# Moving the stores of two output tensors from SP's queue to ScalarE's, in a hybrid decoder layer

## The chip, the cores and the metric

The kernel runs on one core of one Trainium2 chip. The metric is device time in microseconds of one execution, and lower is better. Engines are named as the profile names them: PE is TensorE (its weight loads are listed apart as PEld), DVE is VectorE, ACT is ScalarE, POOL is GpSimd, and SP is SyncE, which here does nothing but issue DMAs.

## The reference

One decoder layer over 2048 tokens of width 1024, in float32. After a norm, one projection feeds two parallel mixers. The first is a diagonal state-space scan with a gated unit behind it; the second a chunked scan over 16 heads with a gate. Each output is normalised, both go through one output projection with a residual, and a gated feed-forward layer follows. Cut to the two places that the change touches:

```python
def s5_mixer(u, ...):
    ...
    g = jax.nn.gelu(y)
    out = g * jax.nn.sigmoid(g @ w_glu + b_glu)       # gated unit

def ssd_mixer(z, xbc, dt, ...):
    ...
    y = (y_diag + y_off).reshape(bsz, L, SSD_HEADS, SSD_HEAD_DIM) + d_skip[:, None] * xh
    y = y.reshape(bsz, L, SSD_WIDTH) * jax.nn.silu(z)

def reference(...):
    y_a = rmsnorm(s5_mixer(...), s5_norm)
    y_b = rmsnorm(ssd_mixer(...), ssd_norm)
    x = x + jnp.concatenate([y_a, y_b], axis=-1) @ w_out
    h = rmsnorm(x, norm_ffn)
    x = x + (silu(h @ w_gate) * (h @ w_up)) @ w_down
    return rmsnorm(x, norm_final)
```

## The kernel before

Float32 products are made of three fp32r matmuls each (high × high, high × low, low × high), so operands are first split into a high part (a cast on ScalarE) and a low part (a subtraction on VectorE or GpSimd). The stages in order: the input projection of the first half of the tokens; tables for the first mixer; the projection of the second half beside the first mixer's scan; then a long stretch in which the second mixer (`ssd`) runs beside the rest of the projection and then beside the gated unit (`glu`), so that PE always has large matmuls to fill the gaps of the mixer's chain; then the output projection and the feed-forward layer as products by Winograd's scheme (`winograd`, L1141).

The second mixer works through four quarters of 512 tokens. In each there are eight pairs of heads, 32 head pairs in all (`ssd_pair`). One pair loads its gate `sz` (L816) and its input `xs` (L818, three buffers), transposes `xs` on PE (`ps_xt`, L822), makes `xde` and `xdt` on VectorE (L827, L828), state products on PE (`ps_st`, L832) and the running state on VectorE (`PV` and `carry`, L840, after a copy on GpSimd, L835); GpSimd makes decay products (L849) that PE sums (`ps_seg`, L850) and ScalarE turns into `L` (exponential, L852); one more exponential makes `E` (L858). PE then makes `ps_yd` (L863) and `ps_yo` (L867). VectorE puts the output together in the tile `E` (L870 to L873), SP stores it to `ybD` (L874), ScalarE squares it (L878) and GpSimd adds the squares up for the norm (L880). `E` has two buffers.

The gated unit works through two halves of 1024 tokens. At the start of each, sixteen loads bring `gD` into staging tiles (L942, a ring of two buffers, `wst`, which the weights use as well), ScalarE casts (L943) and VectorE subtracts (L944). Then come 16 products per half of 24 matmuls (L81 to L83, `ps_glu`), with the weights split at L64 to L69. For each product SP loads `gs` (L955, four buffers), ScalarE takes a tanh (L961, `sg`, two buffers), VectorE multiplies (L962), SP stores `sg` to `yaD` (L963), ScalarE squares it (L965), and GpSimd or VectorE adds the squares up (L967).

No order is written out by hand for most of this. The program's own scheduler, which plays a timeline of the engines through, places every instruction of an engine in a fixed order; the order is then run in order by each engine, and a DMA that waits holds all that stands behind it in its queue. Two rules tie the stages: the matmuls of the gated unit may not be placed before marks in the head pairs (`issue_after`, `k.marks`), two marks to a pair, and the last four products of the 32 stand behind the last mark. DMAs take eight completion semaphores in turn, over both hardware queues together, and a DMA waits until the last one on its semaphore has landed, where that isn't known from another wait.

The output projection takes its first buffers from the space that the second mixer frees, so its splits (L988 on ScalarE, L993 on VectorE) can't start before the last head pair is done. Its operands: `wA` are pieces of the token tile (L1280) and `wS` sums of them (L1099 to L1105); `s` are pieces of the weights (L1270).

Of the kernel before, what the change touches and what calls it, by code (L numbers as in the profile page):

```python
# [58 lines left out]
def split_w(k, src, n=P, lo_pool=False):  # L59

    nc = k.nc
    kt = src.shape[0] // P
    st = k.wp.tile([P, kt, n], F32, tag="wst", name="wst", bufs=k.wst_bufs)
    nc.sync.dma_start(st, src.rearrange("(k p) n -> p k n", p=P))  # L64
    hi = k.wp.tile([P, kt, n], F32R, tag="whi", name="whi", bufs=2)
    nc.scalar.copy(hi, st)  # L66
    lo = k.wp.tile([P, kt, n], F32R, tag="wlo", name="wlo", bufs=2)
    eng = nc.gpsimd if lo_pool else nc.vector
    eng.tensor_sub(lo, st, hi.bitcast(F32))  # L69
    return hi, lo  # L70


def gemm_cm(k, ps, w, r, behind=None):


    nc = k.nc
    (wh, wl), (rh, rl) = w, r
    n = wh.shape[1]
    for i in range(n):
        with k.tc.issue_after(behind[2 * i // n]) if behind else nullcontext():  # L80
            nc.tensor.matmul(ps, wh[:, i, :], rh[:, i, :], start=(i == 0), stop=False)  # L81
            nc.tensor.matmul(ps, wh[:, i, :], rl[:, i, :], start=False, stop=False)  # L82
            last = nc.tensor.matmul(ps, wl[:, i, :], rh[:, i, :], start=False, stop=(i == n - 1))  # L83
    return last
# [189 lines left out]
def bc(ap, shape):  # L274
    return ap.to_broadcast(shape)
# [532 lines left out]
def ssd_pair(k, q, m, grp, d):  # L808

    nc, sp = k.nc, k.sp  # L810
    V, G = nc.vector, nc.gpsimd
    C, Bt, Gm = grp
    cols = slice(q * 512, q * 512 + 512)
    mp = slice(m * P, m * P + P)
    sz = sp.tile([P, 512], F32, name="sz", bufs=2)
    nc.sync.dma_start(sz, k.zD[mp, cols])  # L816
    xs = sp.tile([P, 512], F32, name="xs", bufs=3)
    nc.sync.dma_start(xs, k.xD[mp, cols])  # L818
    hs = slice(2 * m, 2 * m + 2)
    ps = k.ps_x.tile([P, 4, 2, 64], F32, tag="x", name="ps_xt")  # L820
    for i in range(4):
        t = nc.tensor.transpose(ps[:, i].rearrange("p a b -> p (a b)"), xs[:, i * P : i * P + P], k.ident)  # L822
    k.marks.append(t.ins)
    sh = [P, 4, 2, 64]
    xdt = sp.tile(sh, F32, name="xdt", bufs=2)
    xde = sp.tile(sh, F32, name="xde", bufs=1)
    V.tensor_mul(xde, ps, bc(d.ddt[:, :, hs].unsqueeze(3), sh))  # L827
    V.tensor_mul(xdt, ps, bc(d.dtp[:, :, hs].unsqueeze(3), sh))  # L828

    pst = k.ps_x.tile([P, 4, P], F32, tag="x", name="ps_st")  # L830
    for i in range(4):
        nc.tensor.matmul(pst[:, i, :], Bt[:, i, :], xde[:, i].rearrange("p a b -> p (a b)"), start=True, stop=True)  # L832
    PV = sp.tile([P, 4, P], F32, name="PV", bufs=2)
    st = k.carry[:, m, :]
    G.tensor_copy(PV[:, 0, :], st)  # L835
    for i in range(4):
        for hh in range(2):
            s = slice(hh * 64, hh * 64 + 64)
            et = d.etot[:, i, 2 * m + hh : 2 * m + hh + 1]
            V.scalar_tensor_tensor(PV[:, i + 1, s] if i < 3 else st[:, s], PV[:, i, s], et, pst[:, i, s], op0=MUL, op1=ADD)  # L840

    Ls = []
    for hh in range(2):
        psg = k.ps_x.tile([P, 4, P], F32, tag="x", name="ps_seg")
        for i in range(2):
            r = k.r[:, k.turn % 8]
            k.turn += 1
            part = d.dtas[:, i, :, 2 * m + hh : 2 * m + hh + 1].bitcast(F32)
            G.tensor_mul(r, bc(k.tri.unsqueeze(1), [P, 4, P]), bc(part, [P, 4, P]))  # L849
            nc.tensor.matmul(psg.rearrange("p a b -> p (a b)"), k.strir, r.rearrange("p a b -> p (a b)"), start=(i == 0), stop=(i == 1))  # L850
        L = sp.tile([P, 4, P], F32, name="L", bufs=4)
        nc.scalar.activation(L, psg, AF.Exp)  # L852
        V.tensor_mul(L, L, Gm)
        Ls.append(L)
    pe = k.ps_x.tile([P, 512], F32, tag="x", name="ps_e")
    k.marks.append(nc.tensor.matmul(pe, k.sel[:, m, :], d.ac, start=True, stop=True).ins)
    E = sp.tile([P, 512], F32, name="E", bufs=2)
    nc.scalar.activation(E, pe, AF.Exp)  # L858
    yield
    pyd = k.ps_x.tile([P, 4, P], F32, tag="x", name="ps_yd")  # L860
    for i in range(4):
        for hh, L in enumerate(Ls):
            nc.tensor.matmul(pyd[hh * 64 : hh * 64 + 64, i, :], xdt[:, i, hh, :], L[:, i, :], start=True, stop=True)  # L863

    pyo = k.ps_x.tile([P, 4, P], F32, tag="x", name="ps_yo")
    for i in range(4):
        k.before = nc.tensor.matmul(pyo[:, i, :], PV[:, i, :], C[:, i * P : i * P + P], start=True, stop=True).ins  # L867
    yield
    y = E
    V.tensor_mul(y, E, pyo.rearrange("p a b -> p (a b)"))  # L870
    V.tensor_add(y, y, pyd.rearrange("p a b -> p (a b)"))
    V.scalar_tensor_tensor(y, xs, k.dcol[:, m : m + 1], y, op0=MUL, op1=ADD)
    V.tensor_mul(y, y, sz)  # L873
    nc.sync.dma_start(k.ybD[mp, cols], y)  # L874
    if m == 0:
        k.sums = sp.tile([P, 512], F32, name="sums", bufs=1) if q < 3 else k.mx.tile([P, 512], F32, name="sums", tag="w6", bufs=1)
    sq = PV.rearrange("p a b -> p (a b)") if m else k.sums
    nc.scalar.activation(sq, y, AF.Square)  # L878
    if m:
        G.tensor_add(k.sums, k.sums, sq)  # L880
# [46 lines left out]
def glu(k, ins, half, sp):  # L927

    nc = k.nc
    V = nc.vector  # L930
    w_glu = ins["s5_w_glu"][0]
    g = [[k.slot([P, KD, 512], F32R) for _ in range(2)] for _ in range(2)]

    weights = lambda i: [(m, split_w(k, w_glu[:, m * P : m * P + P], lo_pool=True)) for m in (i, i + 1)]
    pair = weights(0)
    for b in range(2):
        hi, lo = g[b]
        for m in range(0, KD, 2):
            gs = k.wp.tile([P, 2, 512], F32, tag="wst", name="wst", bufs=k.wst_bufs)
            j0 = half * 4 + b * 2  # L940
            for i in range(2):
                nc.sync.dma_start(gs[:, i, :], k.gD[(m + i) * P : (m + i) * P + P, j0 : j0 + 2, :].rearrange("p j c -> p (j c)"))  # L942
            nc.scalar.copy(hi[:, m : m + 2, :], gs)  # L943
            V.tensor_sub(lo[:, m : m + 2, :], gs, hi[:, m : m + 2, :].bitcast(F32))  # L944
    sums = sp.tile([P, 2, 512], F32, name="suma", tag="x1", bufs=2)
    for i in range(0, KD, 2):
        if i:
            pair = weights(i)
        order = [(m, w, b) for m, w in pair for b in range(2)]
        if i == 0 or i == KD - 2:  # L950
            order = [(m, w, b) for b in range(2) for m, w in pair]
        for q, (m, w, b) in enumerate(order):
            gs = sp.tile([P, 512], F32, name="gs", tag="t4", bufs=4)
            part = lambda t: t[m * P : m * P + P, half * 4 + b * 2 : half * 4 + b * 2 + 2, :].rearrange("p j c -> p (j c)")
            nc.sync.dma_start(gs, part(k.gD))  # L955
            ps = k.ps_g.tile([P, 512], F32, tag="g", name="ps_glu")

            n = half * 32 + i * 4 + q * 2
            last = gemm_cm(k, ps, w, g[b], [k.marks[min(63, n + 8 + j)] for j in range(2)])
            sg = sp.tile([P, 512], F32, name="sg", bufs=2)  # L960
            nc.scalar.activation(sg, ps, AF.Tanh, scale=0.5, bias=k.cols[:, C_BGLU + m : C_BGLU + m + 1])  # L961
            V.scalar_tensor_tensor(sg, sg, 1.0, gs, op0=ADD, op1=MUL)  # L962
            nc.sync.dma_start(part(k.yaD), sg)  # L963
            sq = gs if m else sums[:, b]
            nc.scalar.activation(sq, sg, AF.Square)  # L965
            if m:
                (V if half and i == KD - 2 else nc.gpsimd).tensor_add(sums[:, b], sums[:, b], sq)  # L967
            if half and i + q == 1:
                with k.tc.issue_after(last.ins):
                    glu_norm(k, 0, k.suma)  # L970
    k.suma = sums
    if half:
        glu_norm(k, 1, sums)
# [486 lines left out]
def trunk_kernel(ctx, tc, ins, out, dbg=None, upto="all"):  # L1460
# [157 lines left out]
    for half in range(2):  # L1618
        glu(k, ins, half, mx)
# [39 lines left out]
```

## Time and profile before

| | us |
|---|---|
| median of 3 runs | 2890.96 |
| lowest, highest | 2889.64, 2892.86 |
| the profiled execution | 2886.14 |
| its span | 2884.4 |
| PE busy in it | 2767.6 |
| VectorE busy | 1984.5 |
| ScalarE busy | 1127.0 |
| GpSimd busy | 897.8 |
| first and last moved store issued at | 762.3, 1229.5 |

The span runs from the first to the last instruction of the program; the profiled execution's own time is 1.74 us longer. Busy time is what an engine spends in instructions that compute; issuing DMAs is not counted in it. The mean granted clock of PE was 0.985 of full speed. An arrow in a row of waits reads "waited for": the engine, line and tile on the left waited for the one on the right; the numbers are the total in us, how often, and the longest.

### The profile page before, as it was taken

How to read it: one execution, taken by the hardware profiler on the slowest of the kernel's cores; microseconds unless marked ns; L12 is line 12 of the kernel's file. 1: busy time of each engine (PE TensorE's matmuls, PEld its weight loads, DVE VectorE, ACT ScalarE, POOL GpSimd, SP SyncE). 2: the span in 40 equal slices, each digit the busy share in tenths (PEclk: the TensorE clock that was granted, in tenths of full speed). 3: DMA queues.
4: the chain of work that ended last, by engine and by line, in shares of the span. 5: the costliest groups of instructions: out<-in, count | busy, mean ns of one | idle time of the engine just before them, and what ended most of it. 6: DMA issues, size and time to landing. Idle time of an engine off the chain costs nothing. (4 is left out here: it accounts for less than half of the span.)

```text
span 2884.4 us, 36196 instructions
## 1 busy us (share of the span) xinstructions
PE 2767.6 (96%) x13116; PEld 2223.4 (77%) x13116; DVE 1984.5 (69%) x3488; ACT 1127.0 (39%) x1799; POOL 897.8 (31%) x1007
## 2 busy tenths in 40 slices
PE   7999999998999998999998999999999999999998
PEld 6777877676887787888776888887888887878776
DVE  7397319997777888876658655557655556785776
ACT  4234332233555343433435333334333334352443
POOL 2488741212766686300142651021400000000021
PEclk9999999999999999999999999999999999999999
DMA  7378656443445555755664773233532224675653
GB/s 186 94 218 272 227 183 185 147 147 96 127 126 168 172 163 176 252 184 177 192 179 124 238 234 119 81 117 103 197 103 88 75 87 153 238 277 175 219 166 105
DMA packets 337690, 473.39 MB, mean 164 GB/s; under 512 B 34940, under 2 KB 242920, under 8 KB 337512
## 3 DMA queue, kind: packets, MB, share of 16 engines
q1 hardware_dynamic: 303048, 367.00, 40.6%
q0 software_dynamic: 25760, 95.69, 9.9%
q10 hardware_dynamic: 8704, 8.39, 1.0%
q8 instruction: 103, 1.69, 0.2%
q14 instruction: 75, 0.61, 0.1%
HBM read 299.06 MB, written 171.97 MB: 163 GB/s over the span
## 5 line engine op out<-in xcount | busy, mean ns | idle before, releaser
L1141 PE MATMUL ps_w<-s,wS 128*128 128x512 f32 x3936 | 952.8, 396 | 23.7 <-DVE s L993 8.4
L1141 PEld LDWEIGHTS ps_w<-s,wS 128*128 128x128 f32 x3936 | 744.0, 190 | 194.4 <-DVE s L993 10.1
L1141 PE MATMUL ps_w<-s,wA 128*128 128x512 f32 x2952 | 721.2, 394 | 10.0 <-ACT s L988 4.4
L1141 PEld LDWEIGHTS ps_w<-s,wA 128*128 128x128 f32 x2952 | 552.6, 188 | 140.4 <-ACT s L988 7.9
L81 PE MATMUL ps_in<-s,whi 128*128 128x512 f32 x896 | 355.7, 398 | 5.5 <-ACT whi L66 3.0
L83 PE MATMUL ps_in<-s,wlo 128*128 128x512 f32 x896 | 354.1, 397 | 5.3 <-POOL wlo L69 3.7
L82 PE MATMUL ps_in<-s,whi 128*128 128x512 f32 x896 | 355.2, 397 | 0.0
L988 ACT CAST wS<-sum 128x512 fp32r<-128x512 f32 (+1 forms) x336 | 203.9, 611 | 379.6 <-PE ps_w L1141 218.3
L993 DVE TENSOR_TENSOR wS<-sum,wS 128x512 fp32r<-128x512 f32 (+1 forms) x336 | 229.3, 686 | 141.6 <-ACT wS L988 141.0
L988 ACT CAST wA<-s 128x512 fp32r<-128x512 f32 (+1 forms) x252 | 150.1, 610 | 266.6 <-PE ps_w L1141 182.7
L69 POOL TENSOR_TENSOR wlo<-wst,whi 128x1024 fp32r<-128x1024 f32 x52 | 143.9, 2768 | 269.6 <-ACT whi L66 243.0
L1401 POOL DMA_DIRECT2D s<-wdD x21 | 15.7, 751 | 613.3 <-DVE s L993 519.3
L81 PEld LDWEIGHTS ps_in<-s,whi 128*128 128x128 f32 x896 | 169.5, 189 | 47.5 <-issue 5.9
L83 PEld LDWEIGHTS ps_in<-s,wlo 128*128 128x128 f32 x896 | 169.4, 189 | 45.2 <-POOL wlo L69 4.5
L82 PEld LDWEIGHTS ps_in<-s,whi 128*128 128x128 f32 x896 | 169.5, 189 | 39.3 <-issue 5.6
L1150 DVE TENSOR_TENSOR gu<-ps_w,gu 128x512 f32<-128x512 f32 x134 | 92.5, 690 | 139.8 <-PE ps_w L1141 138.2
L993 DVE TENSOR_TENSOR wA<-s,wA 128x512 fp32r<-128x512 f32 (+1 forms) x252 | 167.8, 681 | 10.7 <-ACT wA L988 10.6
L849 POOL TENSOR_TENSOR s<-cm,dtas 128x512 fp32r<-128x512 f32 x128 | 163.1, 1301 | 23.3 <-PE ps_seg L850 23.3
L66 ACT CAST whi<-wst 128x1024 fp32r<-128x1024 f32 x72 | 75.5, 1048 | 177.1 <-PE ps_in L82 121.8
L1158 ACT COPY gu<-ps_w 128x512 f32<-128x512 f32 x134 | 78.4, 585 | 142.8 <-PE ps_w L1141 136.7
L1099 DVE TENSOR_TENSOR sum<-s 128x512 f32<-128x512 f32 (+1 forms) x84 | 57.6, 686 | 101.8 <-DMA s<-ybD 34.4
L1160 DVE TENSOR_TENSOR x<-x,sg 128x512 f32<-128x512 f32 x116 | 80.0, 695 | 63.3 <-ACT sg L1158 36.0
(381 smaller groups left out, 3948.7 us busy)
## 6 DMA issues: line engine op xcount, KB each, us to landing
wst<-in_w_in_dram SPq DMA_DIRECT2D x56, 512.0 KB
s<-in_w_gate_dram SPq DMA_DIRECT2D x22, 1024.0 KB
s<-in_w_up_dram SPq DMA_DIRECT2D x22, 1024.0 KB
wdD<-s POOLq DMA_DIRECT2D x22, 1024.0 KB, 6.2
actD<-gu SPq DMA_DIRECT2D x44, 512.0 KB
woD<-s POOLq DMA_DIRECT2D x16, 1024.0 KB, 7.4
s<-actD SPq DMA_DIRECT2D x16, 1024.0 KB
s<-wdD POOLq DMA_DIRECT2D x14, 1024.0 KB, 9.7
```

What stands on the lines that cost most here:

```text
L66: nc.scalar.copy(hi, st)
L69: eng.tensor_sub(lo, st, hi.bitcast(F32))
L81: nc.tensor.matmul(ps, wh[:, i, :], rh[:, i, :], start=(i == 0), stop=False)
L82: nc.tensor.matmul(ps, wh[:, i, :], rl[:, i, :], start=False, stop=False)
L83: last = nc.tensor.matmul(ps, wl[:, i, :], rh[:, i, :], start=False, stop=(i == n - 1))
L849: G.tensor_mul(r, bc(k.tri.unsqueeze(1), [P, 4, P]), bc(part, [P, 4, P]))
L988: a = k.nc.scalar.copy(op[:, 0], raw)
L993: b = eng.tensor_sub(op[:, 1, part], raw[:, part], op[:, 0, part].bitcast(F32))
L1141: nc.tensor.matmul(ps, a[:, p, i, :], b[:, q, i, :], start=(root == name and i == 0 and p + q == 0), stop=(i == n - 1 and p == 1), skip_gr ...
L1150: V.tensor_add(dst, ps, dst if onto else src)
L1158: nc.scalar.copy(dst, bank[root])
L1160: V.tensor_add(block, block, dst)
```

## The change

Two stores are issued by ScalarE and no longer by SP. Both stand in the program's text right ahead of the square of the same tile. 32 stores of `ybD` and 32 of `yaD`, 256 KB each, are moved.

```diff
@@ ssd_pair
     V.tensor_mul(y, y, sz)
-    nc.sync.dma_start(k.ybD[mp, cols], y)
+    nc.scalar.dma_start(k.ybD[mp, cols], y)
...
     nc.scalar.activation(sq, y, AF.Square)
@@ glu
             V.scalar_tensor_tensor(sg, sg, 1.0, gs, op0=ADD, op1=MUL)
-            nc.sync.dma_start(part(k.yaD), sg)
+            nc.scalar.dma_start(part(k.yaD), sg)
             sq = gs if m else sums[:, b]
             nc.scalar.activation(sq, sg, AF.Square)
```

Since the scheduler places all instructions anew, the order of every engine changes from the first moved store to somewhat behind the last. No instruction of PE, VectorE or GpSimd is added or taken away, and the count of ScalarE's table loads stays at 43.

First ScalarE late in the gated unit, at the last three head pairs. Before, no DMA stands there:

```order
L66 CAST whi<-wst 128x1024
L961 ACTIVATE sg<-ps_glu,cols 128x512
L878 ACTIVATE PV<-E 128x512
L965 ACTIVATE gs<-sg 128x512
L852 ACTIVATE L<-ps_seg 128x512 x2
L858 ACTIVATE E<-ps_e 128x512
L961 ACTIVATE sg<-ps_glu,cols 128x512
L878 ACTIVATE PV<-E 128x512
```

And ScalarE at the same place in the changed program:

```order
L852 ACTIVATE L<-ps_seg 128x512 x2
L858 ACTIVATE E<-ps_e 128x512
L963 DMA yaD<-sg 128x512
L965 ACTIVATE gs<-sg 128x512
L961 ACTIVATE sg<-ps_glu,cols 128x512
L963 DMA yaD<-sg 128x512
L965 ACTIVATE gs<-sg 128x512
L874 DMA ybD<-E 128x512
L878 ACTIVATE PV<-E 128x512
L852 ACTIVATE L<-ps_seg 128x512 x2
L858 ACTIVATE E<-ps_e 128x512
```

Each store stands right in front of the square of its tile here, and the exponentials of the next pair stand behind both; of all 64 stores 57 have their square as the very next instruction.

Then SP at the end of the gated unit and the start of the output projection, as one piece of the difference (`woD` holds the output projection's weights, `yaD` read into `s` is its first token tile):

```order
 L1280 DMA s_10561<-yaD 128x8x256
 L1270 DMA s_10563<-woD 128x4x512 x2
 L1280 DMA s_10561<-yaD 128x8x256
-L963 DMA yaD<-sg 128x512
-L1270 DMA s_10562<-woD 128x4x512
-L955 DMA gs<-gD 128x512
-L1270 DMA s_10562<-woD 128x4x512
-L963 DMA yaD<-sg 128x512
+L1270 DMA s_10562<-woD 128x4x512 x2
 L1328 DMA x_10635<-in_x_dram 128x1024
 L1270 DMA s_10563<-woD 128x4x512
-L963 DMA yaD<-sg 128x512
```

The stores are gone from between the weight loads, and the load of `gs` between them has moved ahead.

Last VectorE in the splits for the first products of the output projection. `wA11` and `wS1` are the token operands of its first two products, `s1`, `s2` and `s3` pieces of the weights. Before:

```order
L993 TENSOR_TENSOR s2_10614<-s6_10563,s2_10614 128x1024
L103 TENSOR_TENSOR nt_9257<-nt_9257,nv_9256 128x4
L993 TENSOR_TENSOR s1_10608<-s6_10563,s1_10608 128x1024
L108 SCALAR_TENSOR_TENSOR yinv_91<-nt_9257,yinv_91 128x4
L993 TENSOR_TENSOR s1_10608<-s6_10563,s1_10608 128x1024
L962 SCALAR_TENSOR_TENSOR sg_10460<-sg_10460,gs_10433 128x512
L102 TENSOR_TENSOR nt_9257<-yinv_91 128x4
L993 TENSOR_TENSOR wA11_10579<-s5_10561,wA11_10579 128x512
L993 TENSOR_TENSOR wS1_10585<-sum_10582,wS1_10585 128x512
```

And VectorE there in the changed program:

```order
L993 TENSOR_TENSOR s1_10608<-s6_10563,s1_10608 128x1024
L967 TENSOR_TENSOR suma_9945<-suma_9945,gs_10433 128x512
L993 TENSOR_TENSOR wA11_10579<-s5_10561,wA11_10579 128x512
L993 TENSOR_TENSOR wS1_10585<-sum_10582,wS1_10585 128x512
L102 TENSOR_TENSOR nt_9257<-ng_9258 128x4
L962 SCALAR_TENSOR_TENSOR sg_10493<-sg_10493,gs_10466 128x512
L993 TENSOR_TENSOR s2_10614<-s6_10563,s2_10614 128x1024 x2
L993 TENSOR_TENSOR wS4_10594<-sum_10591,wS4_10594 128x512
```

`s2` now stands behind `wA11` and `wS1`, where it stood ahead of them. `s3`, the operand of the third product that PE runs there, comes behind all of these in both orders.

On PE the head pairs and the matmuls of the gated unit are interleaved differently. From the last `ps_yo` (L867) to the first `ps_w` (L1141) there were 47 + 76 = 123 matmuls of the gated unit and are now 50 + 46 = 96; ahead of each of the last four head pairs 25 more have been done than before. At the start of the gated unit's second half, the pair that had 33 such matmuls behind its transposes now has 16, and the next one has 47 where it had 32.

## The prediction

> **What bounds the kernel now.** First the head of the page: one engine is nearly always busy.
>
> ```profile
> span 2884.4 us, 36196 instructions
> PE 2767.6 (96%) x13116; PEld 2223.4 (77%) x13116; DVE 1984.5 (69%) x3488; ACT 1127.0 (39%) x1799; POOL 897.8 (31%) x1007
> ```
>
> PE (TensorE) leaves 2884.4 − 2767.6 = 116.8 us idle in all. Then the stretches in which the moved stores run (the first is issued at 762 us, the last at 1229 us). The columns are the stretch, its length, and the busy time of PE, weight loads, DVE, ACT and POOL, with the granted clock and the DMA share at the end.
>
> ```profile
> 740.00:900.00 160.00, 157.56 (x926) 130.38 (x926) 131.48 (x215) 86.42 (x113) 107.33 (x100) 0.99 0.41 122
> 900.00:950.00 50.00, 47.30 (x281) 37.58 (x280) 40.54 (x70) 26.86 (x37) 31.26 (x23) 1.00 0.64 199
> 950.00:1070.00 120.00, 116.23 (x715) 96.60 (x714) 99.87 (x173) 45.03 (x75) 91.45 (x71) 0.99 0.54 161
> 1070.00:1125.00 55.00, 45.91 (x262) 36.49 (x261) 49.56 (x88) 23.20 (x33) 32.70 (x24) 0.97 0.64 191
> 1125.00:1215.00 90.00, 90.00 (x521) 74.72 (x520) 73.08 (x121) 39.36 (x60) 50.84 (x38) 1.00 0.63 207
> 1215.00:1245.00 30.00, 28.51 (x132) 22.98 (x131) 26.33 (x48) 16.72 (x25) 1.58 (x2) 1.00 0.84 295
> ```
>
> PE is idle for 505.00 − 485.51 = 19.5 us here: 2.4 + 2.7 + 3.8 + 9.1 + 0 + 1.5. That is the most that any reordering in this stretch can win, 0.7% of the span, and half of it lies at 1070 to 1125 us, where the second half of the gated unit starts. Last, what PE waits for between 740 and 1240 us (total, times, longest):
>
> ```profile
> PE ps_glu L82 <- DVE s L944: 3.9, 4, 2.2
> PE ps_xt L822 <- DVE carry L840: 3.5, 2, 2.7
> PE ps_yo L867 <- ACT L L852: 3.0, 2, 1.8
> PE ps_xt L822 <- ACT L L852: 2.9, 1, 2.9
> PE ps_glu L81 <- ACT s L943: 2.0, 2, 1.8
> PE ps_w L1141 <- DVE s L993: 1.2, 1, 1.2
> ...
> PE ps_ac L749 <- ACT E L858: 0.5, 1, 0.5
> ```
>
> No DMA is in this list. PE waits for VectorE and ScalarE, so a store that is issued elsewhere can help only through what those two wait for.
>
> **What the move costs on ScalarE.** What one issue takes (shortest/median/longest in ns): the two stores on SP now, then two transfers of one shape, a load on SP and the store that ScalarE already issues.
>
> ```profile
> L874 SPq DMA_DIRECT2D ybD<-E x32: 319/320/1137, 762.3 to 1193.7; - x32
> ...
> L963 SPq DMA_DIRECT2D yaD<-sg x32: 319/320/4651, 938.4 to 1229.5; - x32
> ...
> L534 SPq DMA_DIRECT2D s<-uD x48: 567/572/1456, 418.5 to 584.2; - x48
> ...
> L625 ACTq DMA_DIRECT2D gD<-yg x64: 582/587/1155, 472.3 to 716.2; - x64
> ```
>
> The uD load on SP and the gD store on ScalarE carry 128 KB each in rows of the same cut and take 0.57 and 0.59 us: the issue follows the shape, not the engine. So I take 0.32 us for each moved store, 64 × 0.32 = 20.5 us of ScalarE; the other end, 0.59 each, is 37.8 us. ScalarE is busy for 237.6 of the 505 us, so it has room; what counts is the delay of the work behind each store. The store's main wait is not new on ScalarE: the square right behind it waits for the same VectorE result.
>
> ```profile
> ACT PV L878 <- DVE E L873: 48.3, 15, 4.9
> ACT gs L965 <- DVE sg L962: 36.2, 19, 5.7
> ...
> ACT E L858 <- DMA ybD<-E: 8.8, 7, 2.0
> ...
> POOL sums L880 <- ACT PV L878: 53.5, 18, 8.1
> ```
>
> ScalarE mostly stands ready when E or sg is done (15 and 19 times above), so the store goes out at once and the square starts 0.32 us later. Behind it stand the square, then the two exponentials (L852), E (L858), the tanh (L961) and the weight cast (L66). GpSimd waits for the square (18 times), and its next decay products stand behind that add. PE is held by ScalarE directly in 6 of its waits above (2 + 1 + 2 + 1), and by the state recurrence (L840), which follows GpSimd's copy, in 2. Eight places × 0.32 = 2.6 us if each gets one store in front, 5.1 us with both stores of a pair; nothing if the new order puts them elsewhere. I take +1.5, with 0 and +5.1 as ends. E's buffer is freed by its store (8.8 us of ScalarE waits, 0.5 of them passed on to PE): the store goes out from where ScalarE is instead of where SP is, ±0.5, taken as 0.
>
> There is one new kind of wait. As built, most DMAs also wait for the landing of the one eight places earlier in the program, whichever queue holds it: 33 of the 64 stores on ScalarE now wait for a DMA of SP, and 44 DMAs of SP for a store of ScalarE. In the order the partner stands one to two head pairs earlier, so it should have landed; I take 0 and keep the bad case for the rivals.
>
> **What SP gains.** SP's own waits between 740 and 1240 us, the ones that go (L963, L874) between ones that stay:
>
> ```profile
> SPq L818 <- DVE E L872: 61.3, 20, 7.1
> ...
> SPq L963 <- DVE sg L962: 38.1, 20, 4.4
> ...
> SPq L874 <- DVE E L873: 29.7, 23, 5.2
> SPq L955 <- POOL suma L967: 25.5, 16, 5.2
> ...
> SPq L942 <- DVE s L944: 12.8, 8, 2.6
> ```
>
> SP loses 67.8 us of waits, and the loads behind them (sz L816, gs L955, weights L64, xs L818) may go earlier. But xs still waits for its buffer (61.3 us), gs for its own (25.5), and the loads of gD that feed the gated unit for the two staging buffers that L944 frees (12.8). So freeing SP lets loads run up against their buffers. PE's waits at the two starts of the gated unit (3.9 + 2.0 = 5.9 us) hang on that ring of two; I take −1 of them, with 0 and −5.9 as ends.
>
> [...]
>
> **What the new order costs at the end.** This term weighs most. From the last ps_yo to the first ps_w the order holds 123 matmuls of the gated unit before and 96 now; at each of the last four head pairs 25 more have been done than before. These rows (start, length) show what the old tail covered:
>
> ```profile
> 1186.87 1.16 PE L867 MATMUL ps_yo<-Cc,PV 128*128 128x128 f32 x8
> ...
> 1216.27 0.39 PE L82 MATMUL ps_glu<-s,whi 128*128 128x512 f32 x1
> 1216.50 0.39 PE L83 MATMUL ps_glu<-s,wlo 128*128 128x512 f32 x1
> 1216.72 0.62 PE L1141 MATMUL ps_w<-s,wA 128*128 128x512 f32 x2
> ...
> 1223.63 0.49 PE L1141 MATMUL ps_w<-s,wA 128*128 128x512 f32 x1 [0.26 <-ACT s L988]
> 1225.35 0.98 PE L1141 MATMUL ps_w<-s,wA 128*128 128x512 f32 x3 [1.23 <-DVE s L993]
> ...
> 1191.98 1.67 DVE L873 TENSOR_TENSOR E<-E,sz 128x512 f32<-128x512 f32 x1
> 1195.93 2.79 DVE L962 SCALAR_TENSOR_TENSOR sg<-sg,gs 128x512 f32<-128x512 f32 x1 [2.28 <-ACT sg L961]
> 1198.65 2.35 DVE L993 TENSOR_TENSOR s<-s,s 128x1024 fp32r<-128x1024 f32 x2
> ```
>
> A matmul starts every 0.23 us, so the last pair now ends 25 × 0.23 = 5.75 us later in PE's work, and the tail is as much shorter. The splits for the output projection can't start before that pair ends, and PE already ran into them (0.26 + 1.23 = 1.49 us). Before, the third product found its operand at 1225.35 − 1186.87 = 38.5 us after the last ps_yo began: 11.8 us to the first split, 26.7 of VectorE work. In the new order about 24.5 us of VectorE work stand in front of it (11 half splits, 7 small splits, 5 sums, 5 steps of the gated unit; the estimate uses the old stretch less one L962, two waits and the small steps that moved behind), and the first split should start at 10 to 11.8 us, so it is ready at 34.5 to 36.3. PE arrives at 0.9 + 96 × 0.23 + 0.8 + 24 × 0.23 + 0.8 = 30.1. It waits 4.4 to 6.2 us instead of 1.49: I take +3. The ends are 0 (the splits keep pace) and +5.75 (all of the lost cover).
>
> **The sum.** +1.5 − 1 + 3 = +3.5 us. The profiled execution took 2886.14 us, 2884.4 of them its span, so 2889.6; the three runs had a median of 2890.96, 4.8 above, so the forecast is 2890.96 + 3.5, rounded to 2894. About 0.2%, 5.8 us, is what a measurement can tell from no change: the likeliest is a change too small to see. Its own range goes from 0 − 5.9 + 0 to 5.1 + 0 + 5.75, that is −5.9 to +10.9, or 2885 to 2902.
>
> **Rivals.**
>
> *Slower: the head pairs become ScalarE's chain.* If in the gated stage each pair's two stores (0.64 us) go through to GpSimd, VectorE and PE, because the pair's chain and not PE sets the pace, 16 pairs cost 10.2 us; with the tail +13.2, 2899 against the profiled time and 2904 as a median. A store held by a slow load of SP, with the exponentials behind it, would do the same. For it: 1070 to 1125 us, where PE is busy 45.9 of 55 us and DVE 49.6, and the 18 waits of GpSimd. Against it: 1125 to 1215 us, where PE has no idle time at all. It decides from the point where PE waits at L822 or L867 in most pairs. Chance 0.26.
>
> *Faster: inputs and outputs apart.* If the loads of gD do come sooner, the 5.9 us at the two starts go, and the output projection's loads are no longer held by stores of sg (one held SP for 4651 ns), so the 1.49 us go too: −7.4, 2878.7 and 2884. For it: the 67.8 us of SP's waits. Against it: the buffers above. [...] Chance 0.20.
>
> *Nothing: stores were in nobody's way.* ScalarE's slack hides the issues and the splits keep pace: 2886.1 and 2891. Chance 0.18.
>
> **How the numbers follow.** The forecast has 0.36, of which 0.05 lies beyond +5.8 us. Slower by over 0.2%: 0.25 of the first rival + 0.05 = 0.30. Faster: 0.20. Between: 0.31 + 0.18 + 0.01 = 0.50. The range takes in the faster rival's 2884 with some room for a start that goes wholly, and the slower one's up to just short of its 2904: 2882 to 2903.
>
> **What would show it.** The ScalarE rows of L874 and L963 should read about 320 ns; near 590, the first cost doubles. L878 and L965 should keep their VectorE waits, now in front of the store. PE's wait on L993 at the first ps_w should grow from 1.2 to some 4 or 5 us: if it stays at 1.5, the tail term is wrong. If the waits on L944 and L943 (5.9 us) vanish, the buffers were not what held the loads. If PE's waits at L822 and L867 grow well above their 9.4 us, the slower rival is right.

## The result and the profile after

The changed kernel takes 2904.3 us (median of six runs, 2895.84 to 2913.53), the kernel before 2889.3 on the same chip (six runs, 2887.99 to 2892.86). The ratio is 1.0053, 95% interval 1.0040 to 1.0066: slower by 15 us, where 2894.0 was forecast, within 2882 to 2903.

The profiled execution took 2904.32 us. The head of its page:

```profile
span 2902.4 us, 36173 instructions
...
PE 2778.1 (96%) x13116; PEld 2230.3 (77%) x13116; DVE 1984.6 (68%) x3488; ACT 1127.8 (39%) x1799; POOL 908.5 (31%) x1007
```

The span grew by 18.0 us, in two parts that want different explanations. PE's idle time is 2902.4 − 2778.1 = 124.3 us, 7.5 more than before. PE's busy time grew by 10.5 us for the same 13116 matmuls: they ran slower, though 3.4 of these 10.5 us lie ahead of 740 us, where the two programs are the same. The same stretches as before, with the granted clock third from the end of each row:

```profile
740.00:900.00 160.00, 154.61 (x911) 127.91 (x910) 131.10 (x219) 86.75 (x112) 113.03 (x100) 0.99 0.40 121
900.00:950.00 50.00, 47.62 (x279) 38.61 (x279) 37.38 (x60) 26.13 (x37) 28.98 (x23) 0.97 0.61 189
950.00:1070.00 120.00, 116.29 (x697) 96.02 (x696) 98.30 (x169) 44.07 (x73) 84.45 (x67) 1.00 0.53 155
1070.00:1125.00 55.00, 45.02 (x261) 36.72 (x260) 46.12 (x81) 21.82 (x31) 33.20 (x25) 0.94 0.67 199
1125.00:1215.00 90.00, 89.14 (x532) 73.66 (x531) 70.66 (x117) 35.46 (x56) 55.91 (x42) 1.00 0.54 161
1215.00:1245.00 30.00, 23.51 (x93) 18.01 (x92) 28.12 (x47) 18.95 (x27) 1.58 (x2) 0.89 1.00 352
```

PE is idle for 505.00 − 476.18 = 28.8 us here, 9.3 more. The last row changed most: 6.5 us of idle where 1.5 was, and a clock of 0.89 where 1.00 was. PE's work there, start and length, with the wait ahead of it in brackets (`ps_ss`, L920, is the sum for a norm):

```profile
1223.50 0.73 PE L1141 MATMUL ps_w<-s,wA 128*128 128x512 f32 x2 [0.43 <-ACT wA L988]
...
1225.81 1.05 PE L920 MATMUL ps_ss<-cm,suma 128*128 128x1 f32 x8 [1.06 <-DVE suma L967]
...
1233.39 0.49 PE L1141 MATMUL ps_w<-s,wA 128*128 128x512 f32 x1 [1.76 <-ACT s L988]
1237.12 9.58 PE L1141 MATMUL ps_w<-s,wA 128*128 128x512 f32 x30 [3.24 <-DVE s L993]
```

And the same place in steps of 5 us:

```profile
1230.00:1235.00 5.00, 2.13 (x8) 1.16 (x7) 5.00 (x9) 4.45 (x6) 0.00 (x0) 1.00 1.04 393
1235.00:1240.00 5.00, 2.88 (x7) 2.30 (x8) 5.00 (x9) 1.69 (x2) 0.00 (x0) 0.55 1.07 375
1240.00:1245.00 5.00, 5.00 (x19) 3.98 (x18) 5.00 (x10) 2.54 (x5) 1.58 (x2) 0.77 0.70 217
```

The waits are followed by a clock of 0.55 and 0.77. In the last line PE is busy for all of the 5 us and still slow. The clock record has 0.5 from 1235.5 to 1242.3 us: 1.65 us of that lie inside the last wait, and behind it twelve matmuls start 0.39 to 0.59 us apart, most of them 0.43, where 0.23 is usual, which makes 2.5 us in all. The issues themselves (shortest, median and longest in ns) take nearly what was forecast; the waits on E's store and PE's wait on E are what grew:

```profile
L874 ACTq DMA_DIRECT2D ybD<-E x32: 325/353/357, 763.1 to 1208.1; - x32
L963 ACTq DMA_DIRECT2D yaD<-sg x32: 326/326/353, 944.2 to 1238.9; - x32
```

```profile
POOL sums L880 <- ACT PV L878: 52.4, 16, 8.5
ACT PV L878 <- DVE E L873: 43.0, 16, 5.7
ACT E L858 <- DMA ybD<-E: 34.5, 19, 5.8
...
PE ps_g L803 <- ACT E L858: 6.3, 4, 3.5
...
PE ps_yo L867 <- ACT L L852: 4.4, 2, 2.3
...
PE ps_glu L82 <- DVE s L944: 4.2, 4, 2.7
...
ACT whi L66 <- DMA Cc<-xD: 3.7, 1, 3.7
...
PE ps_w L1141 <- DVE s L993: 3.2, 1, 3.2
...
PE ps_xt L822 <- DVE carry L840: 2.9, 1, 2.9
```

E waits for its store for 34.5 us (8.8 before), and PE waits for E with ps_g (L803, the products at the start of each group of four pairs) for 6.3 us, a row that was not there. That made the first theory.

### The profile page after: what moved, and what is told of

Its sections match the earlier page's. It is cut to its first block, busy times and chain, and to the rows that moved or that the text cites. A ratio compares the mean times of both kernels' runs of the same rounds, so it can differ in the third digit from the quotient of the medians.

```text
span 2902.4 us, 36173 instructions
## 1 busy us (share of the span) xinstructions
PE 2778.1 (96%) x13116; PEld 2230.3 (77%) x13116; DVE 1984.6 (68%) x3488; ACT 1127.8 (39%) x1799; POOL 908.5 (31%) x1007
## 5 line engine op out<-in xcount | busy, mean ns | idle before, releaser
L1141 PE MATMUL ps_w<-s,wS 128*128 128x512 f32 x3936 | 951.9, 395 | 23.3 <-DVE s L993 8.0
L1141 PEld LDWEIGHTS ps_w<-s,wS 128*128 128x128 f32 x3936 | 743.0, 190 | 193.8 <-DVE s L993 9.7
L1141 PE MATMUL ps_w<-s,wA 128*128 128x512 f32 x2952 | 726.5, 397 | 16.4 <-ACT s L988 5.9
L1141 PEld LDWEIGHTS ps_w<-s,wA 128*128 128x128 f32 x2952 | 557.0, 190 | 148.4 <-ACT s L988 9.5
L988 ACT CAST wS<-sum 128x512 fp32r<-128x512 f32 (+1 forms) x336 | 204.1, 611 | 372.2 <-PE ps_w L1141 210.9
L993 DVE TENSOR_TENSOR wS<-sum,wS 128x512 fp32r<-128x512 f32 (+1 forms) x336 | 230.4, 689 | 136.4 <-ACT wS L988 135.8
L988 ACT CAST wA<-s 128x512 fp32r<-128x512 f32 (+1 forms) x252 | 150.1, 610 | 276.0 <-PE ps_w L1141 173.7
L993 DVE TENSOR_TENSOR wA<-s,wA 128x512 fp32r<-128x512 f32 (+1 forms) x252 | 168.9, 686 | 11.8 <-ACT wA L988 11.7
L1160 DVE TENSOR_TENSOR x<-x,sg 128x512 f32<-128x512 f32 x116 | 79.2, 688 | 65.0 <-ACT sg L1158 34.5
```

The source lines that it names most:

```text
L988: a = k.nc.scalar.copy(op[:, 0], raw)
L993: b = eng.tensor_sub(op[:, 1, part], raw[:, part], op[:, 0, part].bitcast(F32))
L1141: nc.tensor.matmul(ps, a[:, p, i, :], b[:, q, i, :], start=(root == name and i == 0 and p + q == 0), stop=(i == n - 1 and p == 1), skip_gr ...
L1160: V.tensor_add(block, block, dst)
```

## The experiments

**Theories.** *Buffer*: E is freed by its store, the store on ScalarE lands later, and E's wait holds ScalarE and PE. *Order*: the scheduler's new places cost it, the shorter tail (96 matmuls of the gated unit and not 123 between the last ps_yo and the first ps_w) above all. *Issue*: ScalarE's time for 64 issues. Ratios are to the kernel before, timed on the same chip in the same rounds, with 95% intervals; 0.001 is 2.9 us.

**The order and the queue taken apart.** A table of instruction orders, laid over the program, ties each instruction to the one ahead of it on its engine; so the order of one kernel can be run with the stores of the other.

```diff
     with _tile.TileContext(nc, schedule_with_timeline_sim=True) as tc:
         trunk_kernel(tc, args, out)
+        keep_order(tc)
```

Stores on SP, all else in the new order:

> Stores back on SP, but every other instruction of all five engines in the order of the changed kernel (a table of orders pins it). Three theories of the 15 us by which the changed kernel is slower (2904.3 against 2889.3). Queue: E (two buffers) is freed by its store, the store on ScalarE goes out later and lands later, E's exponential waits for it (34.5 us instead of 8.8) and holds ScalarE; then this kernel is as fast as before, 2889 to 2892, and the waits of E on ybD fall back to some 9 us. Order: the new places of the filler matmuls and the 27 matmuls less in the tail cost it, whoever stores; then 2900 to 2904. Issue: 64 x 0.33 us on ScalarE, passed on; then 2889 to 2892 as well.

Measured: 1.0025 (1.0012 to 1.0038). Stores on ScalarE, all else in the old order:

> Stores on ScalarE, 63 of 64 right in front of their square, but every other instruction of all five engines in the order of the kernel before. Queue: E still waits for its store, 30 us or more, and the time is 2899 to 2905. Order: 2889 to 2893. Issue: 5 to 15 us slower, with E's waits for the store near 9 us and no wait of ScalarE above 1 us added.

Measured: 1.0020 (1.0012 to 1.0028). Neither the queue nor the order is all of it; the two parts, 7 and 6 us, add up to nearly the whole 15. Then one store at a time, order left to the scheduler:

```diff
-    nc.sync.dma_start(k.ybD[mp, cols], y)
+    nc.scalar.dma_start(k.ybD[mp, cols], y)
```

> Only the 32 stores of ybD (from E) are on ScalarE; those of yaD stay on SP, the order is the scheduler's own (96 matmuls of the gated unit in the tail, as in the changed kernel). Queue: nearly all of the loss, 2898 to 2905, E's waits for its store 25 us or more. Issue: half of it, 2896 to 2898. Order: as the changed kernel where the tail counts, 2892 at least, 2904 at most.

Measured: 1.0059 (1.0047 to 1.0071), with E's waits at 37.2 us. And the other store alone:

```diff
-            nc.sync.dma_start(part(k.yaD), sg)
+            nc.scalar.dma_start(part(k.yaD), sg)
```

> Only the 32 stores of yaD (from sg) are on ScalarE; those of ybD stay on SP, the order is the scheduler's own (117 matmuls of the gated unit in the tail). Queue: E's waits near 9 us and the time 2888 to 2893. Issue: half of the loss, 2896 to 2898. Order: the tail is nearly the old one, so 2889 to 2892.

Measured: 0.9991 (0.9980 to 1.0002). The whole loss comes with ybD; 32 issues more on ScalarE cost nothing by themselves, which is against the plain form of *issue*. E waited 19.6 us here at no loss, the first sign against *buffer*.

**A third buffer for E.**

```diff
-    E = sp.tile([P, 512], F32, name="E", bufs=2)
+    E = sp.tile([P, 512], F32, name="E", bufs=3)
...
-        k.sums = sp.tile([P, 512], F32, name="sums", bufs=1) if q < 3 else ...
+        k.sums = k.cp.tile([P, 512], F32, name="sums", tag="junk", bufs=1) if q < 3 else ...
```

> The changed kernel in its own order on all engines, pinned, with one edit: E has three buffers and not two (the room comes from the sums of the first three quarters, which use the space of the norm's scratch tile). If the loss is E waiting for its store: E's waits on ybD fall from 34.5 us to under 3, PE's waits at L803 go, and the ratio to the kernel before falls from 1.0053 to between 1.000 and 1.0025 (the most that the order alone cost with stores on SP). If it is the issue on ScalarE or the shared completion semaphores: 1.004 to 1.0055, unchanged. If it is the order: at least 1.0025.

Measured: 1.0040 (1.0024 to 1.0056).

> The old order on all engines, stores on ScalarE right in front of their squares, E with three buffers. With two buffers this was 1.0020 times the kernel before. If that part is E's wait (19.2 us of it): 0.9990 to 1.0008. If it is the issue in front of the squares or the shared semaphores: 1.0015 to 1.0025 still.

Measured: 1.0012 (1.0001 to 1.0022).

> The kernel before in its own order on all engines, pinned, stores on SP, with E in three buffers: the control for the two others. E waited 8.8 us, 0.5 us of it passed on to PE, so by the buffer theory 0.9990 to 1.0002 times the kernel before; if the third buffer helps here as much as on ScalarE (2 us and more), it is a gain of its own and not the change's price that it takes away.

Measured: 0.9997 (0.9988 to 1.0006).

> The changed kernel with E in three buffers and nothing pinned: the scheduler places everything anew (96 matmuls of the gated unit in the tail, as in the changed kernel). Buffer theory: as the pinned one, 1.000 to 1.0025. Order theory: could be anything from 0.998 to 1.005, and PE's gaps would then lie at other places than in the pinned one. Issue theory: 1.004 or more.

Measured: 1.0035 (1.0021 to 1.0050). In the first of these, E's waits for its store and PE's waits at L803 are gone altogether, and others stand in their place. Three of PE's rows (the first is as it was, the others are longer or new):

```profile
PE ps_yo L867 <- ACT L L852: 4.4, 2, 2.2
PE ps_w L1141 <- ACT s L988: 3.5, 1, 3.5
PE ps_glu L81 <- ACT s L943: 3.3, 1, 3.3
```

The step from two buffers to three is 0.0013 in the new order and 0.0008 in the old one, with intervals that overlap; the control moves by 0.0003. *Buffer* falls as the main cause: a wait of 34.5 us on ScalarE was worth about 4 us by the middle values, a quarter of the loss. Nor does all of that wait come with ScalarE's queue: with the stores on SP in the new order E waited 22.3 us, and with the stores on ScalarE in the old one 19.2.

**The store behind the square.**

```diff
-    nc.scalar.dma_start(k.ybD[mp, cols], y)
...
     nc.scalar.activation(sq, y, AF.Square)
+    nc.scalar.dma_start(k.ybD[mp, cols], y)
```

(the same at L963), first in the old order:

> Stores on ScalarE, each right behind its square and not in front of it; every other instruction of all engines in the old order. In front, this was 1.0020 times the kernel before. If what cost there is the issue that GpSimd's sums wait behind (0.33 us each): 1.0000 to 1.0010. If it is ScalarE's time for the issues as such, or the later landing of E's store: 1.0015 to 1.0030, with E's waits for its store at 19 us or more.

Measured: 0.9994 (0.9985 to 1.0003), though E waits 25.7 us for its store. In front this was 1.0020; the intervals are apart. ScalarE's rows around one square show a difference (ACTq is an issue), first the store in front:

```profile
807.08 0.35 ACTq L874 DMA_DIRECT2D ybD<-E  x1
807.48 0.63 ACT L878 ACTIVATE PV<-E 128x512 f32<-128x512 f32 x1 [0.51 <-DVE E L873]
```

then behind (its square is L877 here and its store L878):

```profile
791.01 0.63 ACT L877 ACTIVATE PV<-E 128x512 f32<-128x512 f32 x1 [2.17 <-DVE E L873]
791.01 0.34 ACTq L878 DMA_DIRECT2D ybD<-E  x1
```

In front, the square starts 0.40 us behind the issue. Behind, issue and square start together, and the 0.34 us lie beside the 0.63 of the square. Over the 32 pairs the square starts 0.43 us (median) after VectorE has made E with the store in front, 0.10 with the store behind, and 0.09 with it on SP.

The same with nothing pinned, then in the changed kernel's order:

> Stores on ScalarE behind their squares, nothing pinned; the scheduler now leaves 131 matmuls of the gated unit for the tail (96 in the changed kernel, 123 before). If the order costs through the tail, that part goes: 0.9995 to 1.0025, with at most 2 us of waits at the first products of the output projection. If the order costs at the starts of the gated unit, it can lie anywhere up to 1.005. If the queue is all: as the one in the old order, 1.001 to 1.003.

Measured: 0.9991 (0.9979 to 1.0003).

> Stores on ScalarE behind their squares, everything else in the order of the changed kernel (96 matmuls of the gated unit in the tail). If the order has a price of its own that adds: 1.0015 to 1.0030, as with the stores on SP (1.0025). If the order costs only together with the place in front: 0.9990 to 1.0008.

Measured: 1.0038 (1.0024 to 1.0052). The order has a price of its own, with the stores on SP or behind the squares. It is above what was expected here, and its interval reaches into that of the changed kernel (1.0040 to 1.0066), so in this order a gain from the place behind is not shown. With the stores behind, the scheduler does not choose that order (131 matmuls stay for the tail).

**The 32 stores of ybD in the old order.**

> Only the 32 stores of ybD on ScalarE, in front of their squares, those of yaD on SP, everything else in the old order. If the part that the queue costs (1.0020 with all 64) comes from the head pairs' chain and E: 1.0012 to 1.0025. If it is ScalarE's time for any issue: half, 1.0005 to 1.0012. If it is the yaD stores that run among the exponentials: 1.0000 to 1.0005.

Measured: 1.0022 (1.0013 to 1.0031): all of the queue's part is ybD's.

**Is it the delay of the square?** The old order, stores on SP, and other work in front of the square:

```diff
+    nc.scalar.copy(k.wait[:, 0:384], y[:, 0:384])
     nc.scalar.activation(sq, y, AF.Square)
```

> The kernel before in its old order, stores on SP; in front of each of the 32 squares of E ScalarE copies 384 columns of E to a scratch tile that nobody reads (about 0.5 us, some 0.4 between starts, as much as a store's issue takes). If a delay of the squares is what the stores in front cost: 1.0012 to 1.0030, as with the ybD stores alone (1.0022). If it is the store's queue, its semaphores or its landing: 0.9993 to 1.0006.

Measured: 1.0009 (1.0000 to 1.0018); the square started 0.45 us after E (median). Twice that work:

> The old order, stores on SP, and two copies of 384 columns of E in front of each of the 32 squares of E, twice the delay (some 0.85 us). If a delayed square is what costs: 1.0015 to 1.0035. If not: 0.9995 to 1.0008.

Measured: 1.0007 (0.9996 to 1.0018). But the edit did not do what was meant. The table of orders does not name the copies, and in the program as built the second one stands behind its square in all 32 cases, as here:

```profile
840.01 0.51 ACT L878 COPY wait<-E 128x384 f32<-128x384 f32 x1 [2.89 <-DVE E L873]
840.43 0.63 ACT L878 ACTIVATE PV<-E 128x512 f32<-128x512 f32 x1
840.96 0.50 ACT L878 COPY wait<-E 128x384 f32<-128x384 f32 x1
```

The square starts 0.45 us after E (median), as with one copy. So the run has the delay once, with more work behind it, and twice the delay was not tried. Then the copy in front with the store behind, on ScalarE:

> The old order, one such copy in front of each square of E, and the stores on ScalarE behind the squares: the square's delay of the changed kernel and its later landing store, but no store in front. If these two together are the price of the place in front: 1.0012 to 1.0030. If the copy alone costs: 1.0003 to 1.0012, as with the stores on SP. If only the store in front itself costs: 0.9990 to 1.0003.

Measured: 0.9996 (0.9986 to 1.0006). Here the square is late by as much and nothing is lost, and the interval is apart from those of the stores in front. With the stores on SP the same delay came to 1.0009 and 1.0007, whose intervals touch those of the stores in front (1.0020 and 1.0022). So the delay is at most part of the 0.0020. What else the place in front does was not found.

**The tail by hand.** The old order, stores on SP; in PE's part of the table 27 matmuls of the gated unit stand among the last pair's ps_yd products and not behind its ps_yo:

```diff
 L863 MATMUL ps_yd<-L,xdt 64x128
 L83 MATMUL ps_glu<-s_9889,wlo 128x512
+L81 MATMUL ps_glu<-s_9889,whi 128x512
+L82 MATMUL ps_glu<-s_9890,whi 128x512
...
 L863 MATMUL ps_yd<-L,xdt 64x128 x7
 L867 MATMUL ps_yo<-Cc,PV 128x128 x4
-L81 MATMUL ps_glu<-s_9889,whi 128x512
-L82 MATMUL ps_glu<-s_9890,whi 128x512
...
```

> The kernel before in its old order, stores on SP, but 27 matmuls of the gated unit stand ahead of the last head pair's ps_yd products and not behind its ps_yo, so that 96 of them are left in the tail as in the changed kernel. If the shorter tail is what the new order costs: PE's waits at the first products of the output projection grow from 1.5 to 4 us or more, with half clock behind them, and the time is 1.0010 to 1.0025. If the new order's price lies elsewhere: 0.9995 to 1.0007.

Measured: 1.0022 (1.0012 to 1.0033), some 6.4 us, nearly what the whole new order costs on SP (1.0025). PE's rows there:

```profile
1203.17 1.05 PE L887 MATMUL ps_ss<-cm,sums 128*128 128x1 f32 x8 [1.35 <-POOL sums L880]
...
1223.67 2.12 PE L1141 MATMUL ps_w<-s,wA 128*128 128x512 f32 x8 [0.54 <-DVE wA L993]
...
1230.84 0.50 PE L1141 MATMUL ps_w<-s,wA 128*128 128x512 f32 x1 [1.35 <-ACT s L988]
1232.56 2.54 PE L1141 MATMUL ps_w<-s,wA 128*128 128x512 f32 x6 [1.22 <-DVE s L993]
```

```profile
1230.00:1235.00 5.00, 2.95 (x8) 2.10 (x9) 5.00 (x7) 4.66 (x7) 0.00 (x0) 0.81 0.91 279
1235.00:1240.00 5.00, 5.00 (x21) 4.06 (x20) 5.00 (x7) 3.78 (x7) 0.00 (x0) 0.85 0.49 160
```

The splits L988 and L993 come late again, and the sum for the norm (L887) too, which the filler had covered; the clock falls to 0.81 and 0.85. With 131 matmuls left (the free kernel with the stores behind), one row has the whole place:

```profile
1215.00:1245.00 30.00, 29.55 (x137) 24.12 (x137) 26.79 (x45) 17.38 (x26) 1.58 (x2) 1.00 0.86 278
```

**Filling the gap.** One try to show the clock's share alone, the changed kernel in its order with matmuls that nothing reads:

```diff
+    for _ in range(20):
+        nc.tensor.matmul(ps, a[:, 0, 0, :], b[:, 0, 0, :], start=True, stop=True, skip_group_check=True)
```

> The changed kernel in its own order on all engines, pinned, with 20 extra matmuls on PE (into the bank of the output projection's third product, ahead of its first real matmul, which overwrites them) where PE waits 1.76 and 3.24 us. They take 20 x 0.23 = 4.5 us and end before the operand is ready, so they delay nothing. If PE's clock is halved because of such gaps: the clock stays at 1.0 from 1230 to 1245 us (0.55 and 0.77 there in the changed kernel) and the 200th matmul of the output projection comes 3.4 us earlier behind the first one, 1.0035 to 1.0048 times the kernel before. If the clock falls for another reason, it falls here too, and the time is that of the changed kernel, 1.0045 to 1.0065.

Measured: 1.0062 (1.0048 to 1.0076). It tells nothing of the clock. The extra matmuls read the first token operand, the cast into a following `wA` tile came at 1239.93 us where it had been at 1231.26, right after they ended, and the operand they were to wait for was late by 8 us:

```profile
1235.03 4.82 PE L1746 MATMUL ps_w<-s,wA 128*128 128x512 f32 x20
1241.55 0.49 PE L1141 MATMUL ps_w<-s,wA 128*128 128x512 f32 x1 [1.70 <-ACT s L988]
```

**All together.** Two sums over each profile, from the fourth pair's ps_xt to the 200th matmul of the output projection: PE's gaps, and, as an estimate of the clock's cost, half of the time that the trace's clock record has at 0.5, split at the last ps_yo into head pairs and tail. In us, from one profile of each kernel; the count is of the gated unit's matmuls in the tail. Where a gap lies inside a stretch at half clock both are counted, which makes a sum too large by up to 2.1 us (0.8 in the changed kernel's tail).

| kernel | matmuls | pairs: gaps, clock | tail: gaps, clock | sum | ratio |
|---|---|---|---|---|---|
| before | 123 | 17.9, 5.1 | 1.5, 0 | 24.5 | 1 |
| changed | 96 | 22.2, 6.8 | 6.5, 3.4 | 39.0 | 1.0053 |
| SP, new order | 96 | 15.0, 10.2 | 3.8, 1.7 | 30.8 | 1.0025 |
| ScalarE, old order | 123 | 22.0, 6.8 | 2.0, 1.7 | 32.5 | 1.0020 |
| ybD alone, free | 96 | 25.8, 6.8 | 4.0, 1.7 | 38.3 | 1.0059 |
| yaD alone, free | 117 | 15.3, 6.8 | 0.7, 0 | 22.8 | 0.9991 |
| changed, three E | 96 | 19.2, 10.2 | 5.5, 3.4 | 38.3 | 1.0040 |
| behind, old order | 123 | 16.5, 5.1 | 1.6, 0 | 23.2 | 0.9994 |
| behind, new order | 96 | 22.7, 6.8 | 4.8, 3.4 | 37.8 | 1.0038 |
| behind, free | 131 | 18.2, 5.1 | 0.9, 0 | 24.2 | 0.9991 |
| short tail by hand | 96 | 16.5, 8.5 | 4.8, 1.7 | 31.5 | 1.0022 |

Every kernel with 96 matmuls in the tail pays 5.5 to 9.9 us there; those with 117 or more pay 0.4 to 3.7 (kernels that the table leaves out are counted). In the changed kernel 8.4 of the 14.5 us that this stretch grew lie in the tail (7.6 without what is counted twice), 6.0 in the pairs. One difference between the dearer and the cheaper of the short tails is a load. In the changed kernel VectorE, which makes the operand that PE waits for, stands still for the first token tile:

```profile
1218.37 0.69 DVE L1099 TENSOR_TENSOR sum<-s 128x512 f32<-128x512 f32 x1 [1.88 <-DMA s<-yaD]
```

The five kernels with 96 matmuls and yaD's stores on ScalarE all have this wait (0.9 to 1.9 us) and pay 7.4 to 9.9 us in the tail; the three with 96 and yaD's stores on SP have none there and pay 5.5 to 6.5. Why the load comes later was not tried. The other 3.5 us of the span lie elsewhere; the half clock ahead of 740 us, where all of these programs are the same, counted in the same way (15.4 us before, 20.5 changed), differs by up to 8.5 us between two profiles, so nothing is built on them.

**A better version.** Stores behind the squares and three buffers for E, nothing pinned (131 matmuls in the tail):

> Stores on ScalarE behind their squares, E in three buffers, nothing pinned (131 matmuls in the tail). With two buffers this was 0.9991, with 41.4 us of E waiting for its store and 6.9 us of PE waiting at L803 for E. If those waits cost what the profile shows: 0.9965 to 0.9980. If they lie beside other waits: 0.9985 to 1.0000.

Measured: 0.9987 (0.9976 to 0.9997), the best of all, by less than the 0.2% that can be told with some safety.

## Why the prediction was wrong, by its own steps

**The tail: the step that failed.** "I take +3. The ends are 0 (the splits keep pace) and +5.75 (all of the lost cover)." The mechanism was right: the 27 matmuls, moved by hand and nothing else, cost 6.4 us (3.5 to 9.5). The wait was near the forecast too: 3.24 us on L993 and 1.76 on L988 at the third product, 5.0 together, where 4.4 to 6.2 was worked out. In part that is luck: the operand was ready 37.9 us after the last ps_yo began, not 34.5 to 36.3, with VectorE's 1.88 us for the token tile in it, and PE was there after 32.5, not 30.1. The term was mis-sized for three reasons. It took 3 where its own numbers gave up to 4.7. It counted one product, while two small waits (0.43 and 1.06) came with it, so that the tail's gaps grew by 5.0 us. And it counted waits only, where a stretch at half clock stood with the wait: of its 6.8 us, 1.65 lie in the wait itself, and the rest cost an estimated 2.6 us more, half of its length (2.5 by the starts of the matmuls). The term should have been about +7.6, above the end that was called all of the lost cover. That the wait brings the half clock is argued from the profiles; no run here shows it alone. In the same order with the stores on SP the tail grew by only 4.0, by hand by 5.0.

**ScalarE's issue, missed by nearly as much.** "I take +1.5, with 0 and +5.1 as ends." The price of one issue was nearly right (0.353 and 0.326 us, where 0.32 was taken), and so was the delay of the square. The old order with the stores on ScalarE costs 5.8 us (3.5 to 8.1), its middle above the upper end. But the reason given, a delay that is passed on at eight places, is at most part of what was found: the same delay by other work gave 2.6 us (0 to 5.2) and 2.0 (−1.2 to 5.2), with the stores behind the squares −1.2 (−4.0 to 1.7), and yaD's 32 issues nothing. That it hangs on the place in front of ybD's squares is shown; by what is open.

**E's buffer.** "±0.5, taken as 0." It was wrong to take the old waits for the new: 8.8 us became 34.5, and 6.3 of them reached PE. The store does not go out later: its issue starts 0.03 us (median) after E is ready in both kernels. Where E waited for it (7 cases before, 19 after), E started 3.3 us after the issue at the earliest with the store on SP and 4.2 with it on ScalarE, but the medians are 4.9 and 5.1: that the store lands later is not shown. Yet taking all of this wait away gave back some 4 us in the new order and 2 in the old: off the path for the most part, though not 0.

**SP.** −1 was about right: PE's waits at the gated unit's two starts fell from 5.9 to 4.2 us, though PE's idle time from 1070 to 1125 us, where the second start lies, grew from 9.1 to 10.0. The loads did run up against their buffers: L955's wait for L967 grew from 25.5 to 63.3 us.

```profile
SPq L955 <- POOL suma L967: 63.3, 17, 10.4
SPq L818 <- DVE E L872: 57.9, 17, 9.0
```

**The shared semaphores.** Taken as 0. Where an order has ScalarE wait for a load of SP there are two rows (3.7 us on Cc, above, and 2.4 on Bc); neither was tried by itself. The first is no price of the stores on ScalarE: with the stores on SP in the same order it stands at 3.5 us.

**The rivals.** The slower rival gave 2904, which is the number that came, by a mechanism that did not: its own test was PE's waits at L822 and L867 growing well above 9.4 us, and they fell to 7.3. The head pairs did lose 6.0 us, but PE's new waits there stand at L803 (6.3 us) and L832 (2.7), so the match of the number is chance. The faster one failed at its buffers, as the evidence against it said.

**The bound.** The idle time of 19.5 us was called "the most that any reordering in this stretch can win". Ahead of the same products an estimated 5.1 us more, half of the 10.2 us at 0.5 in that profile, were lost to half clock; the same holds for what a reordering can lose.

## What to carry to other kernels

When a scheduler places the work anew, look at where the filler ends up before looking at the cost of the instructions that moved: 27 matmuls gone from the cover of a stage's end cost as much as the stores did. Look at the clock record beside a long wait of the matmul engine: in these profiles 58 of its 75 gaps of 2 us or more had a stretch at half clock with them, and such a stretch of 3.4 us cost up to an estimated 1.7, half of its length, with matmuls 0.43 us apart where 0.23 is usual. Try a store that an engine issues itself behind the work that shares its operand and not in front: behind, the issue lay beside that work here (0.34 us beside the 0.63 of the square). In the old order, 1.0020 became 0.9994 by this. And look at the order that was built before reading a run: an instruction that a table of orders does not name can stand anywhere.

## What the runs showed of the hardware

PE's clock was never anything but 1.0 or 0.5 in these records, and the stretches at 0.5 come in steps of 3.4 us (but for the one at the program's end): 3.41, 6.83 and 10.24 us in the profiles of the two kernels. Over the 20 profiles, between 740 and 1260 us, a gap of PE of 2 us or more had such a stretch with it (one that began between 1.5 us before and 3.5 us after the gap's end) in 58 of 75 cases, one of 1.5 to 2 us in 20 of 36, one of 1 to 1.5 us in 8 of 56, a shorter one (0.15 to 1 us) in 9 of 165; 83 of the 86 stretches had a gap of at least 1 us beside them. That goes together; no run here makes a gap alone and shows the clock fall.

What the faster rival stood for, inputs and outputs apart, can be answered for these two outputs: on this kernel moving these two outputs measured 1.0053 (1.0040 to 1.0066) with the stores in front of the squares and 0.9991 (0.9979 to 1.0003) behind them.
